# Subtracting the low parts of the later projection weights on GpSimd instead of VectorE

## The chip, the cores and the metric

One core of one Trainium2 chip. The metric is the device time of one execution of the whole program in microseconds; the kernel before took 951.87 us, the median of three runs from 950.09 to 952.92 us.

## The reference

One layer of a bidirectional hybrid trunk over 640 tokens of width 1024: 128 context tokens and 512 latent tokens. Each token is modulated by adaLN and goes through one combined input projection, whose columns feed three groups: A, differential attention with four heads; B, an HGRN2 gated linear recurrence with four heads and chunks of 64 tokens in both directions; C, grouped-query attention. The results pass one output projection, a LayerNorm, a squared-ReLU MLP and a second LayerNorm.

```
z = (x * (1 + sc1) + sh1) @ w_in            # 640 x 1024 times 1024 x 3328
qa, ka, va, qb, fb_f, fb_b, ib, gb, qc, kc, vc = split(z)
mixed = concat(diff_attention(qa, ka, va), hgrn2(qb, fb_f, fb_b, ib) * silu(gb), gqa(qc, kc, vc))
x = LN(ALPHA * x + g1 * (mixed @ w_out))
x = LN(ALPHA * x + g2 * (relu((x * (1 + sc2) + sh2) @ w_ff1) ** 2 @ w_ff2))
```

The change touches only how the weights `w_in` are prepared for the projections.

## The kernel before

All projections are done in split precision. A float32 operand `src` is split into a high part, a copy rounded to float32r, and a low part, `src - high` (`split`, lines 89 to 91): ScalarE makes the high part, VectorE subtracts. A product is then three matmuls (`mm3`, lines 126 to 130): high times high, high times low, low times high. The activations lie split in `xh` and `xl`.

`wslots` (lines 93 to 124) brings weights in. For each slot it takes a raw buffer `wr`, of which there are two (`NWR`), and a low and a high buffer `wl`, `wh`, of which there are five each (`NWS`); it issues the loads on SP's queue (line 108), and calls `split` on the whole slot, or with `swap=True` on pieces of 256 columns that are rearranged on the way. A raw buffer is free for the next load when both the copy and the subtraction have read it; a high and a low buffer when the matmuls have. A slot holds 768 or 1024 columns per partition.

The callers in the order of the work. In the start stage `first_load` brings `wfq` (gates of the recurrence and first queries), while the adaLN vectors are made. Then `tok_gemm` (line 418) makes the token-major `ib` and `gb`, two slots of 1024 each; `load("fb2")` brings `wfb`, two slots with four pieces of 256 each; `load("q1")` brings `wq`, one slot of 1024. `a_gemm` (line 735) makes queries, keys and values of one head of group A from `wa`, four slots of 768 per head, 16 in all; `c_gemm` (line 845) those of group C from `wc`, four slots of 1024. Later stages load `wo`, `wf` and `wg` by the same function.

Beside the projections runs the recurrence: `gates` and `b_scores` are long sequences of VectorE and ScalarE work over `b_b`, `b_k`, `b_d` and `b_lqk` with small matmuls (`pslv`, `psl`, `pskht`) between, `b_state` a chain of small VectorE steps (line 560). The `ada` calls load further pieces of the adaLN weight and need a ScalarE copy between two matmuls (line 145). The attention follows as a pipeline of units.

The calls from line 1038 on are in an order written out by hand, with projection tiles between the stages of the recurrence. But that order is a priority: a planner lays out the instructions of each engine from these priorities, from the waits for data and free buffers, and from its own estimate of each instruction's cost. Only inside `manual_schedule` blocks is TensorE's order as written. Each engine then takes its instructions strictly in the order laid out. SP's queue holds the loads. GpSimd has little to do: fills of constants and of query tiles, and transfers (small inputs, caches, states in and out, bias rows, context outputs), which it issues itself; such an instruction waits in the queue for what it needs, and what is behind it waits too.

Of the kernel before, what the change touches and what calls it, by code (L numbers as in the profile page):

```python
# [15 lines left out]
ALU = mybir.AluOpType  # L16
# [3 lines left out]
P = 128  # L20
# [33 lines left out]
COL_QA, COL_KA, COL_VA = 0, 512, 1024  # L54
COL_QB, COL_FF, COL_FB, COL_IB = 1536, 1792, 2048, 2304
COL_C = 2816


def f32(ap):
    return ap.bitcast(F32)  # L60
# [3 lines left out]
def hybrid_layer_kernel(ctx: ExitStack, tc: tile.TileContext, T):  # L64
    nc = tc.nc
    V, A, G, PE = nc.vector, nc.scalar, nc.gpsimd, nc.tensor
# [19 lines left out]
    xl = ctile("xl", [P, NK, NTOK], F32R)  # L86


    def split(hi, lo, src):
        A.copy(hi, src)  # L90
        V.tensor_tensor(lo, src, f32(hi), op=ALU.subtract)  # L91

    def wslots(name, src, cols, kper, row0=0, nslot=None, swap=False):


        n = sum(w for _, w in cols)
        nslot = nslot or NK // kper
        out = []
        for s in range(nslot):
            raw = wp.tile([P, kper * n], F32, tag="wr", name=f"{name}_r{s}", bufs=NWR)  # L100
            lo = wp.tile([P, kper * n], F32R, tag="wl", name=f"{name}_l{s}", bufs=NWS)
            hi = wp.tile([P, kper * n], F32R, tag="wh", name=f"{name}_h{s}", bufs=NWS)
            lv = lo.rearrange("p (k n) -> p k n", n=n)
            rv = raw.rearrange("p (k n) -> p k n", n=n)
            off = 0
            r0 = row0 + s * kper * P
            for c0, w in cols:
                nc.sync.dma_start(
                    rv[:, :, off : off + w],
                    src[r0 : r0 + kper * P, c0 : c0 + w].rearrange("(k p) n -> p k n", p=P),  # L110
                )
                off += w
            hv = hi.rearrange("p (k n) -> p k n", n=n)
            if swap:
                for k in range(kper):
                    h_, l_ = (v[:, k, 0:256].rearrange("p (h d c) -> p d h c", d=2, h=2) for v in (hv, lv))
                    split(h_, l_, rv[:, k, 0:256].rearrange("p (d h c) -> p d h c", d=2, h=2))
                if n > 256:
                    split(hv[:, :, 256:n], lv[:, :, 256:n], rv[:, :, 256:n])
            else:  # L120
                split(hi, lo, raw)
            for k in range(kper):
                out.append((hv[:, k, :], lv[:, k, :]))
        return out

    def mm3(ps, s, m, start, stop):

        PE.matmul(ps, s[0], m[0], start=start, stop=False)  # L128
        PE.matmul(ps, s[0], m[1], start=False, stop=False)  # L129
        PE.matmul(ps, s[1], m[0], start=False, stop=stop)  # L130

    def xcols(k, c0, n):
        return (xh[:, k, c0 : c0 + n], xl[:, k, c0 : c0 + n])
# [150 lines left out]
    def ps_mm(name):  # L284
        return pps.tile([P, 512], F32, tag="mm", name=name, bufs=2)
# [7 lines left out]
    def p1t(tag, shape, dtype=F32, bufs=1, name=None):  # L293
        return p1.tile(shape, dtype, tag=tag, name=name or tag, bufs=bufs)
# [121 lines left out]
        V.tensor_tensor(q, q, t, op=ALU.mult)  # L416

    def tok_gemm(name, c0, dst, eng):
        wk = wslots(f"w{name}", T["w_in"], ((c0, 256),), 4)

        def tile_(t):
            ps = ps_mm(f"ps{name}{t}")
            for k in range(NK):
                mm3(ps[:, 0:256], xcols(k, t * P, P), wk[k], k == 0, k == NK - 1)
            eng(dst[:, t, :], ps[:, 0:256])

        return tile_
# [200 lines left out]
    def new_grp(name, par, ck, cv):  # L628
        g = Grp()
        g.name = name  # L630
        g.par = par
        g.qtags = ("a_q0", "a_q1", "b_b1", "b_k1") if name == "C" else ("a_q0", "a_q1", "b_k0", "b_k1")
        g.ltags = ("a_kl", "u6", "u3", "b_b0")
        g.src = (ck, cv)
        g.z = []
        return g
# [7 lines left out]
    def z_tile(g, t):  # L644
        if t == 0:
            return p1t("a_zc", [P, 512], bufs=1, name=f"z{g.name}0")
        if g.par:
            return p1t(f"u{6 + t}", [P, 512], name=f"z{g.name}{t}")
        return p1t("a_z", [P, 512], bufs=4, name=f"z{g.name}{t}")
# [85 lines left out]
    def a_gemm(h):  # L735
        g = new_grp(f"A{h}", h % 2, T["cache_a_k"][:, h * P : (h + 1) * P], T["cache_a_v"][:, h * P : (h + 1) * P])
        g.kcol = P
        g.vcol = 256
        wk = wslots(f"wa{h}", T["w_in"], [(c + h * P, P) for c in (COL_QA, COL_KA, COL_VA)], 2)

        def tile_(t):
            ps = ps_mm(f"psA{h}{t}")
            for k in range(NK):
                mm3(ps[:, 0:384], xcols(k, t * P, P), wk[k], k == 0, k == NK - 1)
            if t == 0:
                z = z_tile(g, t)
                A.copy(z[:, 0:384], ps[:, 0:384])
                nc.gpsimd.dma_start(T["new_a_k"][:, h * P : (h + 1) * P], z[:, P : 2 * P])
                nc.gpsimd.dma_start(T["new_a_v"][:, h * P : (h + 1) * P], z[:, 2 * P : 3 * P])
            else:  # L750
                z = z_tile(g, t)
                rope(z[:, 0:256], ps[:, 0:256], z[:, 256:512], t - 1, 4)
                A.copy(z[:, 256:384], ps[:, 256:384])
            g.z.append(z)

        g.tiles = [lambda t=t: tile_(t) for t in range(NT)]
        return g
# [87 lines left out]
    def c_gemm():  # L845
        g = new_grp("C", 0, T["cache_c_k"], T["cache_c_v"])
        g.kcol = 256
        g.vcol = 384
        wk = wslots("wc", T["w_in"], ((COL_C, 512),), 2)

        def tile_(t):
            ps = ps_mm(f"psC{t}")
            for k in range(NK):
                mm3(ps, xcols(k, t * P, P), wk[k], k == 0, k == NK - 1)
            sq = p1t("tmp", [P, GMAX], bufs=3, name=f"csq{t}")
            ss = p1t("c_ss", [P, 6], bufs=2, name=f"css{t}")
            A.activation(sq, ps[:, 0:384], AF.Square)
            V.tensor_reduce(ss, sq.rearrange("p (g v) -> p g v", v=HD), axis=AX.X, op=ALU.add)
            A.activation(ss, ss, AF.Ln, scale=1.0 / HD, bias=eps)
            A.activation(ss, ss, AF.Exp, scale=-0.5)  # L860
            if t == 0:
                z = z_tile(g, t)
                zn = z[:, 0:384]
            else:
                z = z_tile(g, t)
                zt = p1t("tmp", [P, GMAX], bufs=3, name=f"zn{t}")
                zn = zt[:, 0:384]
            V.tensor_tensor(zn.rearrange("p (g v) -> p g v", v=HD), ps[:, 0:384].rearrange("p (g v) -> p g v", v=HD),
                            ss.rearrange("p (g o) -> p g o", o=1).to_broadcast([P, 6, HD]), op=ALU.mult)
            for lo, n, gg in ((0, 4, qng), (256, 2, kng)):  # L870
                zz = zn[:, lo : lo + n * HD].rearrange("p (g v) -> p g v", v=HD)
                V.tensor_tensor(zz, zz, gg.rearrange("p (o v) -> p o v", o=1).to_broadcast([P, n, HD]), op=ALU.mult)
            if t == 0:
                A.copy(z[:, 384:512], ps[:, 384:512])
                nc.gpsimd.dma_start(T["new_c_k"], z[:, 256:384])
                nc.gpsimd.dma_start(T["new_c_v"], z[:, 384:512])
            else:
                rt = p1t("tmp", [P, GMAX], bufs=3, name=f"rt{t}")
                rope(z[:, 0:384], zn, rt, t - 1, 6)
                A.copy(z[:, 384:512], ps[:, 384:512])  # L880
            g.z.append(z)

        g.tiles = [lambda t=t: tile_(t) for t in range(NT)]
        return g
# [105 lines left out]
    gr, parts, tok, wks = {}, {}, {}, {}  # L990
# [3 lines left out]

    def load(name):
        if name == "q1":
            wks[name] = wslots("wq1", T["w_in"], ((COL_QB + P, P),), 8)
        elif name == "fb2":
            wks[name] = wslots("wfb2", T["w_in"], ((COL_FF + P, P), (COL_FB + P, P)), 4, swap=True)
        elif name == "ib":  # L1000
            tok[name] = tok_gemm("ib", COL_IB, ib, A.copy)
        elif name == "gb":
            tok[name] = tok_gemm("gb", COL_IB + 256, gb, A.copy)
        else:
            gr[0] = a_gemm(0)
# [87 lines left out]
    for h in range(NHA):  # L1093
        for t in range(1, NT):
            n = h * nu + t - 1
# [42 lines left out]
    for t in range(1, NT):  # L1138
        for j in range(4):
            n = NHA * nu + (t - 1) * 4 + j  # L1140
# [96 lines left out]
    for n in range(2):  # L1237
        g1r = gate_rows("g1", n)
        wk = wslots(f"wo{n}", T["w_out"], ((n * 512, 512),), 2)
# [64 lines left out]
    for n in range(2):  # L1304
# [3 lines left out]
        for s in range(NF // 2):  # L1308
            wk = wslots(f"wg{n}_{s}", T["w_ff2"], ((n * 512, 512),), 2, row0=s * 256, nslot=1)
# [99 lines left out]
```

## Time and profile before

| | us |
|---|---|
| median of three runs | 951.87 |
| the profiled execution | 952.96 |
| its span in the trace | 951.2 |
| TensorE (PE) busy, share of the span | 96% |
| VectorE (DVE) busy | 60% |
| ScalarE (ACT) busy | 45% |
| GpSimd (POOL) busy | 6% |

The profiled execution took 1.76 us more than its span, work that lies before the first and behind the last instruction of the trace, and 1.09 us more than the median. A busy share is an average over stages with different limits; the MLP, which takes the second half of the span, is nearly all matmuls. Times of single rows are counted from the start of the span.

### The profile page before, as it was taken

The numbers are of one execution on the slowest core, as the hardware profiler recorded it, in microseconds if no ns is written. First come the engines' busy times: TensorE is split into PE (matmuls) and PEld (weight loads), VectorE is DVE, ScalarE is ACT, GpSimd is POOL, SyncE is SP. The second block draws the span as 40 slices with busy tenths as digits, with TensorE's granted clock in tenths as the row PEclk, the third lists the DMA queues.
The fourth block names the chain that finished last, engine by engine and source line by source line (L and its number), as shares of the span: only waits on it lengthen the run. The fifth ranks groups of instructions, "written<-read, shape, count | busy, mean of one in ns | idle before, by whom it ended". The sixth has DMA issues, their size and how long they took to land.

```text
span 951.2 us, 15540 instructions
## 1 busy us (share of the span) xinstructions
PE 912.9 (96%) x6133; PEld 792.2 (83%) x6133; DVE 573.6 (60%) x1123; ACT 432.7 (45%) x916; POOL 53.5 (6%) x108
## 2 busy tenths in 40 slices
PE   6989898999999998999999999999999999999996
PEld 4778886889889786678899999999998888888884
DVE  2378998988876888873794313243236343563448
ACT  3566675466664657651583212222225333243320
POOL 2200010210100000001000000000000000000000
PEclk9998999999999998999999999999999999999998
DMA  9951525433021320113223234342122222142102
GB/s 260 290 157 54 157 86 162 108 92 94 19 78 39 117 65 13 68 45 133 89 68 111 61 95 133 121 125 73 61 90 84 72 68 88 34 152 80 67 23 88
DMA packets 95752, 90.82 MB, mean 95 GB/s; under 512 B 5792, under 2 KB 81280, under 8 KB 95680
## 3 DMA queue, kind: packets, MB, share of 16 engines
q1 hardware_dynamic: 91936, 82.50, 28.9%
q0 software_dynamic: 3552, 7.27, 2.5%
q8 instruction: 48, 0.79, 0.3%
q14 instruction: 24, 0.20, 0.1%
q10 hardware_dynamic: 192, 0.08, 0.0%
HBM read 86.41 MB, written 3.41 MB: 94 GB/s over the span
## 4 chain that ended last, share of the span: by engine, by line
PE 80%; DVE 11%; ACT 3%; DMA 3%; issue 1%; SPq 1%; DVEq 0%; ACTq 0%
PE psf L1271 8%; PE psy L130 8%; PE psf L1272 8%; PE psf L1273 8%; PE psy L129 8%; PE psy L128 8%; PE psA L129 2%; PE psA L130 2%; PE psavA L730 2%; PE psA L128 2%; PE pswo L130 2%; PE pswo L129 2%; PE pswo L128 2%; DVE b_st L560 2%; PE psavC L952 2%
## 5 line engine op out<-in xcount | busy, mean ns | idle before, releaser
L1271 PE MATMUL psf<-xh,wf_h 128*128 128x320 f32 x512 | 158.7, 310 | 0.0
L1272 PE MATMUL psf<-xl,wf_h 128*128 128x320 f32 x512 | 158.1, 309 | 0.0
L1273 PE MATMUL psf<-xh,wf_l 128*128 128x320 f32 x512 | 158.1, 309 | 0.0
L130 PE MATMUL psy<-wg_h,xl 128*128 128x512 f32 x320 | 127.7, 399 | 0.0
L129 PE MATMUL psy<-wg_l,xh 128*128 128x512 f32 x320 | 126.1, 394 | 0.0
L128 PE MATMUL psy<-wg_h,xh 128*128 128x512 f32 x320 | 125.5, 392 | 0.0
L91 DVE TENSOR_TENSOR xl<-hid,xh 128x640 fp32r<-128x640 f32 x64 | 52.1, 824 | 86.5 <-ACT xh L90 86.5
L90 ACT CAST xh<-hid 128x640 fp32r<-128x640 f32 x64 | 45.6, 727 | 121.7 <-PE psy L129 116.2
L1271 PEld LDWEIGHTS psf<-xh,wf_h 128*128 128x128 f32 x512 | 96.3, 188 | 1.7 <-issue 1.2
L1272 PEld LDWEIGHTS psf<-xl,wf_h 128*128 128x128 f32 x512 | 96.3, 188 | 0.0
L1273 PEld LDWEIGHTS psf<-xh,wf_l 128*128 128x128 f32 x512 | 96.3, 188 | 0.0
L1276 DVE TENSOR_TENSOR hid<-hid,psf 128x320 f32<-128x320 f32 x64 | 31.1, 486 | 106.5 <-ACT hid L1275 106.4
L1275 ACT ACTIVATE hid<-psf 128x320 f32<-128x320 f32 x64 | 28.0, 438 | 119.9 <-PE psf L1273 119.9
L129 PEld LDWEIGHTS psy<-wg_l,xh 128*128 128x128 f32 x320 | 60.1, 188 | 15.6
L128 PEld LDWEIGHTS psy<-wg_h,xh 128*128 128x128 f32 x320 | 60.1, 188 | 14.3
L130 PEld LDWEIGHTS psy<-wg_h,xl 128*128 128x128 f32 x320 | 60.1, 188 | 13.7
L91 DVE TENSOR_TENSOR wf_l<-wf_r,wf_h 128x1024 fp32r<-128x1024 f32 x32 | 39.2, 1224 | 37.5 <-ACT wf_h L90 37.5
L128 PE MATMUL psA<-wa_h,xh 128*128 128x384 f32 x160 | 55.2, 346 | 0.0
L130 PE MATMUL psA<-wa_h,xl 128*128 128x384 f32 x160 | 54.9, 344 | 0.0
L129 PE MATMUL psA<-wa_l,xh 128*128 128x384 f32 x160 | 54.7, 343 | 0.0
L90 ACT CAST wf_h<-wf_r 128x1024 fp32r<-128x1024 f32 x32 | 33.7, 1054 | 32.8 <-PE psf L1272 28.4
L91 DVE TENSOR_TENSOR wg_l<-wg_r,wg_h 128x1024 fp32r<-128x1024 f32 x32 | 39.2, 1224 | 7.1 <-ACT wg_h L90 4.5
(475 smaller groups left out, 1897.2 us busy)
## 6 DMA issues: line engine op xcount, KB each, us to landing
wad<-in_w_ada SPq DMA_DIRECT2D x32, 512.0 KB, 4.8
wf_r<-in_w_ff SPq DMA_DIRECT2D x32, 512.0 KB, 3.9
wg_r<-in_w_ff SPq DMA_DIRECT2D x32, 512.0 KB, 3.6
adaw<-in_w_ada SPq DMA_DIRECT2D x32, 256.0 KB, 5.4
wa_r<-in_w_in SPq DMA_DIRECT2D x48, 128.0 KB, 2.9
wo_r<-in_w_out SPq DMA_DIRECT2D x8, 512.0 KB, 3.7
x<-in_x_sample SPq DMA_DIRECT2D x8, 256.0 KB, 4.9
wc_r<-in_w_in SPq DMA_DIRECT2D x4, 512.0 KB, 3.7
```

Of the source, the lines that this page charges most:

```text
L90: A.copy(hi, src)
L91: V.tensor_tensor(lo, src, f32(hi), op=ALU.subtract)
L128: PE.matmul(ps, s[0], m[0], start=start, stop=False)
L129: PE.matmul(ps, s[0], m[1], start=False, stop=False)
L130: PE.matmul(ps, s[1], m[0], start=False, stop=stop)
L560: V.scalar_tensor_tensor(dst, st[r, c, :], dec[r, c : c + 1], u(r, c), op0=ALU.mult, op1=ALU.add)
L730: PE.matmul(po, pT[:, c, :], vals(g, c, c0, n), start=(c == 0), stop=(c == NKC - 1))
L1271: PE.matmul(ps[:, 0:HALF], h, xh[:, k, sl], start=(k == 0), stop=False)
L1272: PE.matmul(ps[:, 0:HALF], h, xl[:, k, sl], start=False, stop=False)
L1273: PE.matmul(ps[:, 0:HALF], l, xh[:, k, sl], start=False, stop=(k == NK - 1))
L1275: A.activation(hs, ps[:, 0:HALF], AF.Relu)
L1276: V.tensor_tensor(hs, hs, ps[:, 0:HALF], op=ALU.mult)
```

## The change

`split` and `wslots` get a parameter `eng`, the engine of the subtraction; without it VectorE is used as before. The five calls, for `ib` and `gb` together, `wa`, `wc`, `wq` and `wfb`, pass GpSimd. The high part is made on ScalarE as before, and `wfq`, `wo`, `wf`, `wg` and the activations are split as before.

```diff
-    def split(hi, lo, src):
+    def split(hi, lo, src, eng=None):
         A.copy(hi, src)
-        V.tensor_tensor(lo, src, f32(hi), op=ALU.subtract)
+        (eng or V).tensor_tensor(lo, src, f32(hi), op=ALU.subtract)
...
-    def wslots(name, src, cols, kper, row0=0, nslot=None, swap=False):
+    def wslots(name, src, cols, kper, row0=0, nslot=None, swap=False, eng=None):
...
-                    split(h_, l_, rv[:, k, 0:256].rearrange("p (d h c) -> p d h c", d=2, h=2))
+                    split(h_, l_, rv[:, k, 0:256].rearrange("p (d h c) -> p d h c", d=2, h=2), eng)
                 if n > 256:
-                    split(hv[:, :, 256:n], lv[:, :, 256:n], rv[:, :, 256:n])
+                    split(hv[:, :, 256:n], lv[:, :, 256:n], rv[:, :, 256:n], eng)
             else:
-                split(hi, lo, raw)
+                split(hi, lo, raw, eng)
...
-        wk = wslots(f"w{name}", T["w_in"], ((c0, 256),), 4)
+        wk = wslots(f"w{name}", T["w_in"], ((c0, 256),), 4, eng=G)
...
-        wk = wslots(f"wa{h}", T["w_in"], [(c + h * P, P) for c in (COL_QA, COL_KA, COL_VA)], 2)
+        wk = wslots(f"wa{h}", T["w_in"], [(c + h * P, P) for c in (COL_QA, COL_KA, COL_VA)], 2, eng=G)
...
-        wk = wslots("wc", T["w_in"], ((COL_C, 512),), 2)
+        wk = wslots("wc", T["w_in"], ((COL_C, 512),), 2, eng=G)
...
-            wks[name] = wslots("wq1", T["w_in"], ((COL_QB + P, P),), 8)
+            wks[name] = wslots("wq1", T["w_in"], ((COL_QB + P, P),), 8, eng=G)
         elif name == "fb2":
-            wks[name] = wslots("wfb2", T["w_in"], ((COL_FF + P, P), (COL_FB + P, P)), 4, swap=True)
+            wks[name] = wslots("wfb2", T["w_in"], ((COL_FF + P, P), (COL_FB + P, P)), 4, swap=True, eng=G)
```

## Rows read from the trace of the kernel before

**Rows 1.** The page's engine totals: busy us, share of the span, instructions.

```profile
PE 912.9 (96%) x6133; PEld 792.2 (83%) x6133; DVE 573.6 (60%) x1123; ACT 432.7 (45%) x916; POOL 53.5 (6%) x108
```

**Rows 2.** Busy time by stretch: length, each engine's busy us, granted clock, DMA share, GB/s.

```profile
95.00:120.00 25.00, 22.57 (x217) 20.66 (x216) 24.17 (x64) 16.65 (x44) 1.51 (x2) 0.93 0.54 167
...
245.00:270.00 25.00, 24.56 (x163) 22.64 (x161) 19.75 (x43) 12.17 (x36) 1.43 (x2) 1.00 0.10 28
```

**Rows 3.** What TensorE waited for: us in total, times, longest us.

```profile
PE pskht L488 <- DVE b_kq L485: 3.1, 1, 3.1
PE psl L499 <- DVE b_k L528: 2.4, 1, 2.4
PE psada L976 <- ACT ada L145: 2.2, 1, 2.2
```

**Rows 4.** Subtractions of line 91 that move: duration ns min/median/max, first and last start.

```profile
L91 DVE TENSOR_TENSOR wa_l<-wa_r,wa_h x16: 936/951/960, 143.2 to 279.7; 128x768 fp32r<-128x768 f32 x16
...
L91 DVE TENSOR_TENSOR wfb_l<-wfb_r,wfb_h x8: 415/418/425, 63.4 to 85.9; 128x256 fp32r<-128x256 f32 x8
...
L91 DVE TENSOR_TENSOR wc_l<-wc_r,wc_h x4: 1218/1221/1227, 284.6 to 318.4; 128x1024 fp32r<-128x1024 f32 x4
L91 DVE TENSOR_TENSOR wib_l<-wib_r,wib_h x2: 1224/1224/1225, 52.3 to 54.8; 128x1024 fp32r<-128x1024 f32 x2
L91 DVE TENSOR_TENSOR wgb_l<-wgb_r,wgb_h x2: 1209/1213/1217, 95.8 to 103.5; 128x1024 fp32r<-128x1024 f32 x2
L91 DVE TENSOR_TENSOR wq_l<-wq_r,wq_h x1: 1215/1215/1215, 91.6 to 91.6; 128x1024 fp32r<-128x1024 f32 x1
```

**Rows 5.** Groups of GpSimd's instructions by form: busy us, mean ns, idle before.

```profile
L432 POOL MEMSET b_lqk<- 128x768 f32 x3 | 2.2, 739 | 22.2 <-PE psada_s L143 22.2
...
L254 POOL CAST masks<-mf 128x256 uint8<-128x256 f32 x1 | 0.4, 396 | 1.8 <-DMA mf<-in_k_masks 1.8
...
L960 POOL MEMSET brow<- 128x256 f32 x1 | 0.3, 330 | 0.0
```

**Rows 6.** Timelines of GpSimd, and of VectorE at 110 us: start, us, instruction.

```profile
110.29 0.77 POOL L569 DMA_DIRECT2D out_new_state_fwd<-b_stn  x1 [24.24 <-DVE b_stn L560]
111.05 0.75 POOL L570 DMA_DIRECT2D out_new_state_bwd<-b_stn  x1
...
136.88 0.55 POOL L569 DMA_DIRECT2D out_new_state_fwd<-b_stn  x1 [4.51 <-DVE b_stn L560]
...
110.34 0.61 DVE L388 TENSOR_SCALAR mixed<-mixed,lbt 128x640 f32<-128x640 f32 x1
```

**Rows 7.** The chain that ended last, 52 to 71 us: start, us, what.

```profile
52.29 1.24 DVE wib_l L91
53.54 0.37 SPq L108
...
57.23 5.68 DMA wfb_r<-in_w_in
...
65.03 0.42 DVE wfb_l L91
...
70.62 0.33 DVE wfb_l L91
```

**Rows 8.** What VectorE waited for, 75 to 95 us, then 145 to 175 us.

```profile
DVE b_att L538 <- ACT b_att L537: 1.5, 1, 1.5
DVE b_att L539 <- PE psl L499: 1.0, 1, 1.0
...
DVE sc L978 <- ACT wa_h L90: 1.4, 1, 1.4
DVE ada L147 <- PE psadag L143: 1.3, 1, 1.3
DVE sc L978 <- PE psada L976: 0.8, 2, 0.6
```

**Rows 9.** A weight load of TensorE's that waited for a low part.

```profile
PEld psC L129 <- DVE wc_l L91: 0.2, 1, 0.2
```

**Rows 10.** Busy time by stretch, 112.5 to 115 us; columns as in rows 2.

```profile
112.50:115.00 2.50, 2.50 (x11) 2.50 (x11) 2.47 (x5) 2.35 (x8) 0.00 (x0) 0.50 0.03 7
```

## The prediction

> **What bounds the kernel now.** The page's engine totals come first [rows 1]: TensorE is busy 912.9 of 951.2 us, VectorE 60%, GpSimd 6%. So all that a change off TensorE can win is in the 38 us in which TensorE has nothing to do, and in stretches in which its clock is lowered. The average hides that the work has stages, so the second view is the busy time by stretch [rows 2]. From 95 to 120 us, in the HGRN2 part, VectorE is busy 24.17 of 25 us while TensorE has 2.4 us of gaps: there VectorE sets the pace. From 245 to 270 us, in the attention part, TensorE is busy 24.56 of 25 and VectorE 19.75: there TensorE sets it, and a lighter VectorE buys next to nothing. The third view is what TensorE waits for [rows 3]: 3.1 us for `b_kq` at 71 us, 2.4 us for `b_k` at 111 us, both from VectorE, and 2.2 us for ScalarE's `ada` copy, which stands behind a ScalarE instruction that VectorE feeds. These three are what the change can shorten or lengthen.
>
> **What moves.** The subtractions of line 91 for six weight names go from VectorE to GpSimd [rows 4]: 2 of `wib` and 2 of `wgb` and 1 of `wq` and 4 of `wc` at 1.21 to 1.22 us each, 8 of `wfb` at 0.42, 16 of `wa` at 0.95. That is 9 x 1.22 + 8 x 0.42 + 16 x 0.95 = 29.5 us off VectorE. The cast to the high part stays on ScalarE, the loads stay on SP's queue, no instruction is added. The subtractions of `wfq`, `wo`, `wf`, `wg` and of the activations stay on VectorE.
>
> **What one costs on GpSimd.** No subtraction ran there before, so I bound it. Two fills give the cost of one pass [rows 5]: (739 - 330) / 512 = 0.80 ns an element, 0.125 us fixed. One pass over 1024 elements is 0.94 us, the lower bound. Two reads and a write done as three passes are 2.58 us for 1024, 1.97 for 768, 0.74 for 256, the upper bound. The cast of 256 elements at 396 ns shows that a read beside a write is cheaper than a pass of its own, but it writes single bytes; I take the upper bound. So each result comes about twice as late after its cast as on VectorE, if nothing stands before it. [...]
>
> **What it costs VectorE while it runs.** This decides the sign, and no row shows it, since GpSimd never read two tiles before. The lower bound is nothing. The upper bound is that VectorE stands still for the whole subtraction, as nearly all that it runs in these stretches reads two SBUF tiles or streams one at speed. The nearest row is a small one [rows 6]: GpSimd's two output transfers of a state take 0.77 and 0.75 us beside VectorE's `TENSOR_SCALAR` at 110.34 us, but 0.55 us at 136.88. The two engines do get in each other's way; I take the upper bound, in which a subtraction of 1.22 us on VectorE turns into a stop of 2.58. [...]
>
> **The sum, in three places.**
>
> *A, 52 to 71 us.* The chain of waits [rows 7] runs through this change: `wib_l` ends at 53.54, frees a raw buffer (there are two, `NWR`), and at that moment SP issues the `wfb` load; SP's constants follow in order, the other `wfb` loads go at 57.23 and land 5.68 us later, and everything to the 3.1 us wait hangs on that. The subtraction takes 2.58 instead of 1.22, so this starts 1.36 us later. Two `wfb_l` subtractions, 0.42 and 0.33 us, leave the chain. Net +0.6 us. Behind the waiting SP instruction stand the constants and the `ada` weight loads, which are needed later.
>
> *C, 72 to 112 us.* Off VectorE: 5 x 0.42 of `wfb`, 1.22 of `wq`, 2 x 1.21 of `wgb`, together 5.7 us. Added as stops: 5 x 0.74 + 3 x 2.58 = 11.4 us. VectorE's own idle time there can swallow 1.5 + 1.0 us [rows 8]. Net 11.4 - 2.5 - 5.7 = +3.2 us, and all of it lengthens TensorE's 2.4 us wait, since TensorE has run out of filler matmuls by then.
>
> *D, 141 to 157 us.* Four `wa` subtractions: off 4 x 0.95 = 3.8, added 4 x 1.97 = 7.9, idle to swallow it 1.4 + 1.3 + 0.8 = 3.5 [rows 8]. Net +0.6 us on the chain that feeds the `ada` copy.
>
> Elsewhere I cost the change at nothing: the other twelve `wa` and the four `wc` run beside an attention stage whose matmuls cover both VectorE's relief and its stops. If that cover fails, the price is a low part that reaches TensorE late: 1.36 us for a `wc`, 1.02 for a `wa`. One row shows that this is near, a weight load that already waits 0.2 us for `wc_l` [rows 9].
>
> GpSimd's own queue is nearly empty (53.5 us in all [rows 1]). What now stands behind a subtraction are fills for the query tiles and transfers of caches, states and bias rows, each up to 2.6 us later, which has slack. The reverse, a subtraction behind a GpSimd instruction that itself waits, can cost far more (one waited 24.24 us [rows 6]); the planner orders queues by its own estimate of when things are ready, so I leave it to the range. So do I with the changed order of all engines: the planner sees other costs and will place matmuls differently after 52 us.
>
> Sum: 0.6 + 3.2 + 0.6 = +4.4 us on the profiled execution's 952.96 us, 957.4. The median of the runs is 1.09 us below that execution, so **956.3 us**.
>
> **Rivals.**
> *VectorE is not held at all (faster).* [...] With A's +0.6: -5.1 us, 946.7. For it: VectorE is the pacing engine there and GpSimd idle. Against: the lengthened transfers. It begins to decide where the stops of C fall under what is removed and swallowed, 5.7 + 2.5 = 8.2 us of the 11.4. Chance 0.34.
>
> *VectorE is held only while GpSimd reads.* Two passes of three: C's stops are 7.6 us, 0.6 less than what is removed and swallowed; D comes out covered; A's +0.6 stays. Sum 0.0, 951.9. Chance 0.24. What would be late next is the same `b_k`, hardly moved.
>
> *The held case with late low parts.* The forecast plus one `wc` and one `wa` late, 1.36 + 1.02: 958.7. Chance 0.10; the forecast by itself 0.32.
>
> **How the numbers follow.** About 0.3%, 2.9 us, can be told from no change. Slower by more: 0.32 + 0.10 = 0.42. Within it: 0.24. Faster: 0.34. Low end: the first rival, with a GpSimd subtraction at its one-pass bound so that A turns from +0.6 to -1.0, 945.1; I say 945. High end: 958.7 and the 1.25 us of lowered clock twice more, after the two waits that grow, 961.2; I say 961. Both signs hold most of the chance; the forecast's own range is 954 to 961.
>
> **What would show it.** Right: VectorE's two-input instructions between 85 and 105 us (scans, `b_lqk`) grow by up to 2.6 us wherever a GpSimd subtraction runs beside them; the wait of TensorE for `b_k` near 111 us grows from 2.4 to over 5; the `wfb` loads leave SP some 1.4 us later; a GpSimd subtraction of 1024 takes 2 us or more. Wrong: VectorE's instructions keep their lengths beside GpSimd's subtractions, its busy total falls by the full 29.5 us, and the `b_k` wait is gone; or the planner's order changes so much that TensorE's gaps lie in other places.

## The result, and the profile after

The changed kernel takes **978.1 us** (median of four runs, 976.9 to 980.3) against 952.4 before in the same job: ratio 1.0274, 95% interval 1.0249 to 1.0299. It is slower, as forecast, but by 25.7 us where the sum had 4.4, and outside the range of 945 to 961.

The page's totals of the changed kernel answer to [rows 1].

```profile
PE 920.8 (94%) x6133; PEld 798.3 (82%) x6133; DVE 571.1 (58%) x1090; ACT 435.0 (45%) x916; POOL 114.5 (12%) x141
```

33 instructions and 29.5 us of subtractions have left VectorE, and its busy time fell by 2.5 us: 573.6 - 29.5 = 544.1, so 27.0 us came back. Summed one by one, the VectorE instructions that stayed are 23.6 us longer; the rest is that instructions in a row overlap a little, which the busy time counts once: 47.3 us of VectorE's instructions overlap before, 43.9 after. The span grew by 25.1 us, of which TensorE has 7.9 more busy and 17.2 more idle.

Next, the moved subtractions but for `wq_l`, by source line and operation (duration min/median/max in ns, first and last start), against [rows 4].

```profile
L91 POOL TENSOR_TENSOR wa_l<-wa_r,wa_h x16: 1804/1824/2407, 150.4 to 298.7; 128x768 fp32r<-128x768 f32 x16
L91 POOL TENSOR_TENSOR wfb_l<-wfb_r,wfb_h x8: 719/862/1916, 65.6 to 77.7; 128x256 fp32r<-128x256 f32 x8
L91 POOL TENSOR_TENSOR wc_l<-wc_r,wc_h x4: 2334/2384/2432, 300.5 to 338.4; 128x1024 fp32r<-128x1024 f32 x4
L91 POOL TENSOR_TENSOR wib_l<-wib_r,wib_h x2: 2382/2386/2389, 52.7 to 58.4; 128x1024 fp32r<-128x1024 f32 x2
L91 POOL TENSOR_TENSOR wgb_l<-wgb_r,wgb_h x2: 2687/2698/2708, 94.5 to 99.3; 128x1024 fp32r<-128x1024 f32 x2
```

The timelines of GpSimd and of VectorE from 90 to 104 us show where that comes from (start, us, instruction).

```profile
90.73 2.39 POOL L91 TENSOR_TENSOR wq_l<-wq_r,wq_h 128x1024 fp32r<-128x1024 f32 x1
94.48 2.71 POOL L91 TENSOR_TENSOR wgb_l<-wgb_r,wgb_h 128x1024 fp32r<-128x1024 f32 x1 [1.35 <-ACT wgb_h L90]
99.33 2.69 POOL L91 TENSOR_TENSOR wgb_l<-wgb_r,wgb_h 128x1024 fp32r<-128x1024 f32 x1 [2.14 <-ACT wgb_h L90]
...
90.76 2.72 DVE L388 TENSOR_SCALAR b_b<-b_b,lbt 128x640 f32<-128x640 f32 x1
95.12 2.42 DVE L390 TENSOR_SCALAR b_k<-b_b 128x640 f32<-128x640 f32 x1
98.34 1.48 DVE L392 TENSOR_TENSOR_SCAN b_b<-scanm,b_b 64x640 f32<-64x640 f32 x1
100.50 2.87 DVE L393 TENSOR_TENSOR_SCAN b_b<-scanm,b_b 64x640 f32<-64x640 f32 x1
```

Read them in pairs. Line 388 takes 0.61 us in [rows 6]; here it starts 0.03 us after `wq_l` and ends 0.36 us behind it. Line 390, 0.49 us in the kernel before, ends 0.35 us behind the first `wgb_l`. The scan of line 392 is under way when the second `wgb_l` starts and keeps its 1.48 us; the same scan at line 393, which starts during that subtraction, takes 2.87 and ends 1.35 us behind it.

What TensorE waits for has changed places too (columns as in [rows 3]).

```profile
PE psl L499 <- DVE b_stn L560: 4.9, 2, 4.1
PE pskht L488 <- DVE b_kq L485: 4.7, 2, 4.0
PE psqA L678 <- DVE zA L623: 3.5, 3, 2.2
PE psqA L678 <- DVE lam L355: 3.0, 1, 3.0
...
PE psada L976 <- ACT ada L145: 1.4, 1, 1.4
```

The `psl` products near 120 us no longer wait for `b_k` but for the state steps of line 560; two waits of the first attention head are new. VectorE's queue isn't the old one less 33 instructions: the planner gave every engine another order. First products by stage, before and after: `pskht` 71.3 and 75.6 us, `psq` 104.3 and 112.5, `psA` 152.7 and 165.5, `psC` 313.0 and 337.5, `pswo` 426.1 and 451.3. So 12.8 us are lost before the first attention product, 11.7 between it and `psC`, 0.7 up to `pswo`, nothing behind it.

The first stretch of [rows 2] and the one behind the 4.1 us wait for `b_stn` (columns as there):

```profile
95.00:120.00 25.00, 19.85 (x192) 18.56 (x192) 23.75 (x54) 13.88 (x33) 4.87 (x2) 0.99 0.43 136
...
120.00:125.00 5.00, 4.26 (x29) 4.17 (x30) 4.86 (x12) 2.17 (x7) 1.50 (x2) 0.50 0.04 10
```

From 95 to 120 us TensorE lacks 5.2 us of 25 where it lacked 2.4, and VectorE is as full as before. Behind the long wait the granted clock is 0.50, as it was in [rows 10] behind a shorter one; some of TensorE's extra busy time comes from there: a `psq` product of the changed kernel takes 0.47 us at 123 us and 0.31 at 115 us, where the clock is 1.00.

### The profile page after: what moved, and what is told of

Same layout as the page of the kernel before. It is cut to its first block, busy times and chain, and to the rows that moved or that the text cites. A ratio compares the mean times of both kernels' runs of the same rounds, so it can differ in the third digit from the quotient of the medians.

```text
span 976.3 us, 15559 instructions
## 1 busy us (share of the span) xinstructions
PE 920.8 (94%) x6133; PEld 798.3 (82%) x6133; DVE 571.1 (58%) x1090; ACT 435.0 (45%) x916; POOL 114.5 (12%) x141
## 4 chain that ended last, share of the span: by engine, by line
PE 74%; DVE 11%; issue 6%; ACT 3%; DMA 3%; SPq 1%; POOL 1%; DVEq 0%; ACTq 0%; POOLq 0%
PE psf L1271 8%; PE psy L130 8%; PE psf L1272 8%; PE psf L1273 8%; PE psy L129 8%; PE psy L128 8%; PE psavA L730 2%; PE pswo L130 2%; PE pswo L129 2%; PE pswo L128 2%; PE psavC L952 2%; PE psA L128 2%; PE psA L130 1%; PE psA L129 1%; DVE b_st L560 1%
## 5 line engine op out<-in xcount | busy, mean ns | idle before, releaser
L91 DVE TENSOR_TENSOR wg_l<-wg_r,wg_h 128x1024 fp32r<-128x1024 f32 x32 | 39.2, 1224 | 7.3 <-ACT wg_h L90 4.5
```

The source lines that it names most:

```text
L91: (eng or V).tensor_tensor(lo, src, f32(hi), op=ALU.subtract)
```

## The experiments

Two things changed at once: the engine of 33 instructions, and everybody's order. Both kernels consist of the same instructions, so either can be held to the other's order: each instruction of an engine gets a plain order edge to its predecessor in the wanted list (shortened).

```
+    for i in ORDER:                        # the other kernel's order
+        ins = trace[i]
+        if ins.engine in last:
+            tc.add_manual_dep(ins, last[ins.engine].name, no_sync)
+        last[ins.engine] = ins
```

"Old order" is that of the kernel before, "new order" that of the changed kernel. Losses are differences of medians within one job (the kernel before had 952.3 to 953.5 there).

| run | order | low parts on | median us | ratio, 95% interval | loss us | VectorE busy |
|---|---|---|---|---|---|---|
| before | old | VectorE | 952.4 | | | 573.6 |
| r1 | old | GpSimd | 966.8 | 1.0150 (1.0129-1.0171) | 13.6 | 572.2 |
| r2 | new | VectorE | 971.7 | 1.0203 (1.0181-1.0225) | 18.5 | 575.0 |
| r4 | old | GpSimd, hardly reading | 956.0 | 1.0027 (1.0011-1.0043) | 3.0 | 551.2 |
| r5 | new | GpSimd, hardly reading | 961.1 | 1.0087 (1.0064-1.0109) | 8.0 | 550.3 |
| changed | new | GpSimd | 978.1 | 1.0274 (1.0249-1.0299) | 25.7 | 571.1 |

**r1 and r2: engine or order.**

> The changed kernel (all 33 subtractions on GpSimd), but with every engine's instructions held in the order that the planner had given the kernel before. The changed kernel lost 25.7 us (952.4 to 978.1). Theory 1, the engine alone costs it (VectorE's instructions stretch beside GpSimd's subtractions, low parts and raw buffers come later): the loss stays, 972 to 982 us. Theory 2, the planner's new order of the other instructions costs most: 953 to 962 us, with VectorE's busy time still near 571 us, since the stretch would stay and only stop mattering. If both matter, between 962 and 972.

> The kernel before (all subtractions on VectorE, none on GpSimd), but with every engine's instructions held in the order that the planner gave the changed kernel. Theory 1, engine alone: 950 to 955 us, as the kernel before. Theory 2, order: 968 to 980 us, with TensorE waiting at the same places as in the changed kernel (the subtraction's own state chain b_stn, psqA, pskht) although no VectorE instruction is stretched.

r1 comes out between its two theories, r2 within that of the order. Each alone costs, and together less than their sum, 25.7 against 32.1. Measured from the old order, the engine is 13.6 us and the order another 12.1. r2 has the changed kernel's waits with no subtraction on GpSimd.

```profile
PE psl L499 <- DVE b_stn L560: 4.9, 2, 4.1
PE psqA L678 <- DVE lam L355: 4.5, 1, 4.5
```

These two are the order's. r1 has neither; there `ada` and `b_lqk` lead.

```profile
PE psada L976 <- ACT ada L145: 6.2, 1, 6.2
...
PE pslv L499 <- DVE b_lqk L515: 2.8, 2, 2.2
```

**r3: the pairs by themselves.**

```
+    def y_sub(o): G.tensor_tensor(o, ga, gb, op=ALU.subtract)   # also memset, copy
+    def x_sub(o): V.tensor_tensor(o, va, vb, op=ALU.subtract)   # and six other forms
```

> None of the layer is computed: this kernel only runs six VectorE instructions of each of seven forms, first alone, then beside a stream of GpSimd subtractions (128x1024, both inputs and the output in SBUF), beside GpSimd memsets and beside GpSimd copies; the outputs are filled with zeros. Theory 'held for the whole subtraction' (the upper bound of the prediction): a VectorE instruction with two SBUF inputs takes up to its own time plus about 2.4 us beside the subtractions, and a form with one input or with its input in PSUM keeps its length. Theory 'not held': every form keeps its length within 0.05 us. Theory 'held while reading only': the added time is near 1.6 us of each 2.4. [...]

VectorE's groups by tile (ns min/median/max, first and last start), then the timelines of both engines.

```profile
L82 DVE TENSOR_TENSOR vo_x_sub_alone<-va,vb x6: 1159/1224/1224, 6.8 to 13.9; 128x1024 f32<-128x1024 f32 x6
L82 DVE TENSOR_TENSOR vo_x_sub_y_set<-va,vb x6: 1224/1224/1224, 54.9 to 61.1; 128x1024 f32<-128x1024 f32 x6
L82 DVE TENSOR_TENSOR vo_x_sub_y_sub<-va,vb x6: 1224/3245/3245, 15.7 to 28.1; 128x1024 f32<-128x1024 f32 x6
L94 DVE TENSOR_TENSOR_SCAN vo_x_scan_y_sub<-va,vb x6: 1492/3446/3448, 312.7 to 328.1; 128x640 f32<-128x640 f32 x6
L91 DVE TENSOR_SCALAR vo_x_imm_alone<-va x6: 493/1200/1202, 229.5 to 235.0; 128x640 f32<-128x640 f32 x6
L91 DVE TENSOR_SCALAR vo_x_imm_y_sub<-va x6: 494/2951/3393, 236.1 to 247.2; 128x640 f32<-128x640 f32 x6
```

```profile
3.28 12.04 POOL L106 MEMSET go_x_sub_y_set<- 128x1024 f32 x12
8.93 6.19 DVE L82 TENSOR_TENSOR vo_x_sub_alone<-va,vb 128x1024 f32<-128x1024 f32 x5
...
21.24 2.42 POOL L103 TENSOR_TENSOR go_x_sub_y_sub<-ga,gb 128x1024 f32<-128x1024 f32 x1
23.61 0.95 POOL L106 MEMSET go_x_sub_y_set<- 128x1024 f32 x1
24.52 2.42 POOL L103 TENSOR_TENSOR go_x_sub_y_sub<-ga,gb 128x1024 f32<-128x1024 f32 x1
...
229.94 4.65 POOL L106 MEMSET go_x_imm_y_set<- 128x1024 f32 x4 [1.02 <-ACT t L125]
...
390.50 2.35 POOL L103 TENSOR_TENSOR go_x_psum_y_sub<-ga,gb 128x1024 f32<-128x1024 f32 x1
390.51 4.30 DVE L97 TENSOR_TENSOR vo_x_psum_y_copy<-pt,vb 128x512 f32<-128x512 f32 x6
```

The planner mixed the streams, so the labels don't say what ran beside what; the starts do. The subtractions called "alone" from 8.93 us run beside GpSimd's memsets, those called "y_set" from 54.9 us beside an idle GpSimd: 1224 ns both. Beside GpSimd's subtractions VectorE gets one instruction through for each of GpSimd's: it lasts 3245 ns, 2.02 us more, from 0.26 us behind the subtraction's start, and GpSimd's period (21.24 to 24.52, with a memset in it) is 3.28 us. The scan (1491 ns undisturbed) grows by 1.95 us. The form that reads PSUM keeps its length beside the same subtractions (4.30 us for six from 390.51, under 0.7 each at any time). So "held for the whole subtraction" stands, 2.02 of the 2.33 us that a subtraction takes beside an idle VectorE; "held while reading", with 1.6, falls.

The one-input `TENSOR_SCALAR`, which the prediction's list of signs didn't name and which r3's own theory took to keep its length, is held too: 0.49 us beside an idle GpSimd, up to 3.39 beside its subtractions. It is held by memsets as well: of the six called "alone", the four that run beside GpSimd's memsets from 229.94 us take 1.20 us, and the memsets that meet them 1.18 instead of 0.95. So memsets on GpSimd, which only write, leave VectorE's two-input forms as they are (subtraction 1224 ns, product 824, scan 1491 beside them) and hold this one-input form.

**r4 and r5: GpSimd as long busy, but hardly reading.** Here the low parts are mostly zeros.

```
-        eng.tensor_tensor(lo, src, f32(hi), op=ALU.subtract)
+        eng.tensor_tensor(lo[..., 0:2], src[..., 0:2], f32(hi)[..., 0:2], op=ALU.subtract)
+        eng.memset(f32(lo), 0.0)            # twice
+        eng.tensor_tensor(lo[..., 0:2], src[..., 0:2], f32(hi)[..., 0:2], op=ALU.subtract)
```

> The old order, as in r1, but each GpSimd subtraction is replaced by a tiny one (2 columns of each row), two memsets of the low part and a tiny one again: GpSimd is busy for about as long (2.1 us where the subtraction takes 2.4), low parts and raw buffers are released about as late, but GpSimd hardly reads SBUF; r3 showed VectorE unchanged beside memsets. The low parts are then mostly zeros. Theory 'VectorE held': the 13.6 us of r1 vanish, 948 to 955 us, and VectorE's busy time falls to about 545 us. Theory 'low parts and raw buffers late, GpSimd's queue': 963 to 967 us, as r1.

> The same replacement in the order that the planner gave the changed kernel (978.1 us with the real subtractions; 971.7 with the subtractions on VectorE). Theory 'VectorE held, and the order costs by itself': 964 to 971 us: the holding is gone, the order's loss stays. Theory 'the order costs only because the subtractions sit badly in it': 950 to 957 us. Theory 'late low parts': about 977 us.

```profile
PE 909.2 (95%) x6133; PEld 788.2 (83%) x6133; DVE 551.2 (58%) x1090; ACT 432.7 (45%) x916; POOL 117.5 (12%) x240
...
57.65 2.33 DVE L332 TENSOR_SCALAR sel<-ident,selw 128x128 fp32r<-128x128 f32 x2
...
57.65 2.10 POOL L432 MEMSET b_lqk<- 128x768 f32 x3
```

GpSimd is busy for 117.5 us against 113.4 in r1, VectorE 21.0 us less, and 10.6 of r1's 13.6 us are gone. r4 is 1.0 us above the range of its first theory, and r5, at 961.1, lies between its first two. "VectorE unchanged beside memsets" holds for two-input forms only, so r4 isn't free of holding: VectorE's total is 7.1 us above the 544.1 that the subtractions leave, where the text expected about 545, and 4.9 of that are longer instructions. Most of these are early, two one-input `sel` instructions that take 2.33 us beside the kernel's own `b_lqk` fills where they took 0.48 before. So the holding by subtractions is at least 10.6 us in the old order and 17.7 in the new one, and the new order by itself is 5. The 3.0 us left in r4 are what late low parts and buffers cost, with the holding left, less what VectorE's relief gives; the three weren't measured apart. r4 does say that with low parts as late as that, 22.4 us less of VectorE's time don't make the kernel faster.

**r6, r7, r9: which stage.** r6 moves `wa` and `wc` only, r7 the other three call sites only, r9 is r6 with r4's replacement, all in the old order. The counts in two texts below are off: it is 20 subtractions (16 of `wa`) and 13.

> The old order; of the 33 subtractions only those of the attention stage (12 of wa, 4 of wc) are on GpSimd, the 17 of wib, wfb, wq and wgb stay on VectorE. The prediction counted 0.6 us for these 16 (953.7 us here). Rival: the stage doesn't cover the holding; r1's milestones lose 5 to 7 us between the first wa product and the last wc product, so 958 to 960 us.

> The old order; only the 17 subtractions of wib, wfb, wq and wgb are on GpSimd, those of wa and wc stay on VectorE. The prediction counted 3.8 us (957 us here). Rival, by r1's milestones: 7 to 8 us are lost before the first wa product, so 960 to 962 us. If r6 and r7 add up to r1's 13.6 us, the two stages cost independently.

> As r6 (old order; only the 20 subtractions of wa and wc on GpSimd, 961.1 us), with each of them replaced as in r4 by two tiny subtractions and two memsets, so that GpSimd is as long busy and hardly reads. The low parts of wa and wc are then mostly zeros. Theory 'VectorE held': most of r6's 8.0 us vanish, 952 to 956 us. Theory 'low parts and raw buffers late' in this stage: 959 to 961 us.

r7: 957.0 us, +4.0 (ratio 1.0044, 1.0028 to 1.0059), as the prediction counted. r6: 961.1, +8.0 (1.0088, 1.0065 to 1.0110), 1.1 above its rival's range. r9: 956.4, +2.9 by the medians (1.0045, 1.0027 to 1.0062), 0.4 above its first theory's range. The attention stage is the dearer one, and some 5 of its 8 us are the holding (4 by the ratios). The sum of r6 and r7, 12.0, is within the noise of r1's 13.6. One place shows how it gets to TensorE: first the kernel before, then r6, timelines of three engines near 143 us.

```profile
142.22 1.02 DVE L511 TENSOR_TENSOR b_d<-mixed 128x384 f32<-128x384 f32 x2
...
144.55 0.37 ACT L145 COPY ada<-psada 128x256 f32<-128x256 f32 x1
```

```profile
142.79 4.50 DVE L511 TENSOR_TENSOR b_d<-mixed 128x384 f32<-128x384 f32 x2
...
142.49 2.05 POOL L91 TENSOR_TENSOR wa_l<-wa_r,wa_h 128x768 fp32r<-128x768 f32 x1 [0.97 <-ACT wa_h L90]
...
145.05 1.82 POOL L91 TENSOR_TENSOR wa_l<-wa_r,wa_h 128x768 fp32r<-128x768 f32 x1
...
145.04 0.45 ACT L512 ACTIVATE b_d<-b_d,sgn 128x192 f32<-128x192 f32 x1 [1.69 <-DVE b_d L511]
...
146.73 0.37 ACT L145 COPY ada<-psada 128x256 f32<-128x256 f32 x1
```

Two subtractions `b_d` stand one behind the other on VectorE, and each meets one `wa_l`: 1.02 us become 4.50. ScalarE's next instruction waits 1.69 us for the first, the `ada` copy stands behind it in ScalarE's queue and comes 2.18 us later, and TensorE's wait for `ada` goes from 2.2 to 4.1 us. The first `psA` product starts 3.0 us later than before.

Further on the loss grows where one head of attention follows another. What TensorE waits for (columns as in [rows 3]), in the kernel before, in r6 (with two rows of its timelines) and in r9:

```profile
PE psqA L678 <- DVE zA L623: 0.4, 1, 0.4
```

```profile
PE psqA L678 <- DVE zA L623: 2.1, 2, 1.2
...
PE pssA L705 <- DVE k0A L669: 1.2, 1, 1.2
...
317.05 2.19 DVE L623 TENSOR_TENSOR zA<-zA 128x256 f32<-128x256 f32 x1
...
314.27 4.69 POOL L91 TENSOR_TENSOR wc_l<-wc_r,wc_h 128x1024 fp32r<-128x1024 f32 x2 [12.16 <-ACT wc_h L90]
```

```profile
PE psC L129 <- POOL wc_l L1397: 1.1, 1, 1.1
...
PE psA L129 <- POOL wa_l L1397: 1.0, 1, 1.0
```

The step `zA` takes 0.43 us at this place in the kernel before, 2.19 beside `wc_l`, and the first products of the head wait for it. In r9 the wait for `zA` is 0.4 us again, and TensorE waits 1.1 and 1.0 us for a low part: most of r9's 2.9.

**r11 and r12: the size of a hold, and VectorE's time without one.**

```
+    for c in range(0, m, m // 4):           # r11: four quarters on GpSimd (shortened)
+        eng.tensor_tensor(lo[..., c : c + w], src[..., c : c + w], f32(hi)[..., c : c + w], op=ALU.subtract)
```

```
     V.tensor_tensor(lo, src, f32(hi), op=ALU.subtract)
+    V.tensor_tensor(lo, src, f32(hi), op=ALU.subtract)   # r12: twice on VectorE
```

> As r1 (all 33 subtractions on GpSimd, the old order, 966.8 us), but each subtraction of 1024 or 768 columns is four of 256 or 192, one behind the other; those of 256 stay. Theory 'a VectorE instruction waits for one whole GpSimd instruction': it now waits for about 0.7 us in place of up to 2.4 and slips in between two quarters, so VectorE's added time falls and the kernel takes 956 to 962 us. Rival 'the two share a path and the sum of their reading counts': 966 to 970 us, since GpSimd is as long busy or longer.

> The kernel before (subtractions on VectorE, the old order), with each of the 33 subtractions done twice in a row on VectorE: 29.5 us more of VectorE's time in the places where the subtractions stand, about as much as GpSimd's holding adds in r1 (28 us). Theory 'VectorE is late wherever it is held, and its time in these stages is the bound': 962 to 970 us. Rival 'VectorE has room there, and what costs in r1 is that the holding falls on instructions that others wait for': 953 to 957 us.

r11: 961.2 us (ratio 1.0090, 1.0064 to 1.0116), 5.6 us better than r1, though GpSimd is busy 130.9 us instead of 113.4; VectorE's total falls to 565.2. A hold that is over sooner costs less, and the rival of a shared sum falls. r12: 972.5 us (1.0214, 1.0179 to 1.0250), above both its ranges, VectorE 602.4 us. There 28.8 more us of VectorE's time cost 20.0, 0.7 us for each. So more time on VectorE in these places does go to the end; but r12's low parts also come one subtraction later (TensorE waits 1.7 us for `wa_l`), and that part wasn't taken apart. r1 adds nearly as much by holding (25.2, summed one by one) and takes the 29.5 us of subtractions away, and still loses 13.6: what it takes away pays little of it back.

**r8 and r10: filling single waits.** r8 mends the two waits of the changed kernel that are the order's; r10 does one such edit in the kernel before.

```
 PE (r10):  - psl x16, psq x16     + psq x16, psl x16
 PE (r8):   - psl x16, psq x22     + psq x22, psl x16
 DVE (r8):  - b_st x7, zA/lam x9   + zA/lam x9, b_st x7
```

> The changed kernel with its real subtractions on GpSimd and in its own order, but for two places. The 16 products psl, before which TensorE waits 4.1 us for the state steps b_stn, come 22 psq products later on TensorE; and nine instructions that the first attention queries need (zA and lam) come ahead of the last 7 of the 16 state steps on VectorE, where TensorE waited 3.0 us. Theory 'what the new order costs over the old one (11.3 us with the subtractions on GpSimd) lies in such places': 978.1 minus 4 to 8, so 970 to 974 us. Rival 'the waits only move, since VectorE is behind by as much': 976 to 979 us, with a new wait just behind each place.

> The kernel before (subtractions on VectorE), in its own order but for one place: the 16 products psl, before which TensorE waits 2.4 us for b_k near 111 us and after which its granted clock falls to 0.50, come 16 psq products later. If the wait is filled and the clock doesn't fall there: 948.5 to 951 us. If the time only moves to the wait behind it: 952 to 954 us, as before.

r8 takes 979.2 us (1.0273, 1.0259 to 1.0287), the same as the changed kernel; my theory fell. r10 takes 953.7 (0.9999, 0.9985 to 1.0013). r8's list of TensorE's waits says why: the time has gone next door.

```profile
PE pskht L488 <- DVE b_kq L485: 6.4, 4, 4.0
...
PE psl L499 <- DVE b_k L528: 3.6, 1, 3.6
PE psgb L128 <- ACT b_q L409: 3.2, 1, 3.2
```

In r10 the 2.4 us for `b_k` are gone and the waits for `b_kq` are 6.8 us in place of 3.1; the granted clock is at 0.50 again, from 118 to 121 us. A wait of TensorE's names who came last, not what the time hangs on.

**r13 and r14: whose order.** Both with all low parts on GpSimd; r13 is r1 with the queues of GpSimd and SP in the new order, r14 the changed kernel with these two in the old.

> As r1 (all 33 subtractions on GpSimd; VectorE, ScalarE and TensorE in the old order, 966.8 us), but the queues of GpSimd and of SP run in the order that the planner gave the changed kernel: the first low part stands ahead of the fills of b_lqk and of the state loads, the query fills and output transfers stand between other subtractions. Theory 'the new order costs through the queues': 974 to 978 us, as the changed kernel. Rival 'through the compute engines': 965 to 969 us.

> The counterpart: the changed kernel (978.1 us) with the queues of GpSimd and SP in the old order, VectorE, ScalarE and TensorE in the new one. Theory 'queues': 966 to 970 us. Rival 'compute engines': 976 to 980 us. If neither of r13 and r14 moves by 3 us or more, the cost lies in how the orders of the engines fit each other.

r13: 968.4 us (1.0159, 1.0136 to 1.0181), r14: 985.5 (1.0356, 1.0334 to 1.0379). Losses are 16.0 and 33.1 us: the two queues in the new order cost 2.4 us beside the old order of the rest, which the noise can hide, and save 7.4 beside the new; r14 is above both its ranges. So the order's loss sits with VectorE, ScalarE and TensorE. Their orders were not exchanged one at a time; which of their placements costs the 5 to 12 us stays open.

## Why the prediction was right and wrong

**Right: what a subtraction costs on GpSimd.** Taken 2.58, 1.97 and 0.74 us, measured 2.33, 1.80 and 0.72 at best. Where nothing held it r3 shows 2.33 for 1024. VectorE holds GpSimd as well: 2.69 for `wgb_l`, 1.92 for one `wfb_l`.

**Right: VectorE is held for the whole of it.** r3 (1224 ns become 3245), r4 (10.6 of r1's 13.6 us gone) and r11 (5.6 us less with quarters) show it, against the two rivals that had 0.58 of the chance.

**Right in size, C by luck: A and C.** The other `wfb` loads left SP at 58.72 us in the changed kernel, 1.49 later than in [rows 7] (taken: 1.36), and at 58.12 in r7, 0.89 later. r7 measures A and C together, 4.0 us where the steps had 0.6 + 3.2 = 3.8. The sign by which the loss was to show was wrong: the `b_k` wait did not grow to 5 us; in r7 `b_lqk` (2.2 us) and `b_kq` (4.4 in all) took it, and in the changed kernel `b_k` stands at 1.1. Nor does C's sum hold with what was measured: the VectorE instructions that stand between 72 and 112 us in the kernel before grew by 7.9 us in r7, where the prediction took a stop for each subtraction, 11.4. Its own terms then give 7.9 - 2.5 - 5.7 = -0.3. What cost was where a stop fell: a pair of `b_lqk` steps beside the second `wgb_l` took 2.65 us in place of 0.58, and TensorE waited for that (r7's timeline and waits):

```profile
103.76 2.65 DVE L515 TENSOR_TENSOR b_lqk<-b_k,b_d 64x128 f32<-64x128 f32 x2
...
PE pslv L499 <- DVE b_lqk L515: 2.2, 1, 2.2
```

**Wrong: D and "elsewhere".** "The other twelve `wa` and the four `wc` run beside an attention stage whose matmuls cover both VectorE's relief and its stops", with 0.6 us for the first four. r6 measured 8.0 us for these 20. The idle time that was to swallow the stops in D, 3.5 us in [rows 8], lay mostly at 151 to 162 us, and the first stops fell on `b_d` at 142, ahead of it: +3.0 us instead of +0.6 at the first `psA`. Part of it is won back, since TensorE waits 1.4 us for a weight at 161 us in the kernel before: the first `psqA` starts at 193.8 us before and at 196.0 in r6. The other 6 us come where the prediction had nothing. A stage in which TensorE is 24.56 of 25 us busy [rows 2] is not covered at the changes of head; at those TensorE waits for a short chain on VectorE and ScalarE, and a stop on that chain counts, as `zA` shows. The price put on a failed cover, late low parts for 1.36 + 1.02 us, is near the 2.1 us of such waits in r9; it left out the holding, some 5 us here. This mis-sized term is 7.4 us of the missing 21.3.

**Wrong: the order left to the range.** "So do I with the changed order of all engines", and then the high end had two lowered clocks in it and no order. No run shows the 1.25 us counted for each of the two, an estimate from the 2.5 us at half the clock in [rows 10]; in stretches of 2.5 us the granted clock is at 0.50 for 41.0 us in the changed kernel and for 20.5 before, the end of the span behind the matmuls left out. The order cost 12.1 us on top of r1. With the 1.6 us by which r1 exceeds r6 and r7 together (12.0 against 13.6; r1's interval alone is 2.0 us to each side), the two steps make up the miss: 7.4 + 12.1 + 1.6 = 21.1 of 21.3, and r7's 0.2 is the rest. Which placements in the new order cost this stays open; r13 and r14 leave those of VectorE, ScalarE and TensorE.

**The first rival would have been wrong too.** It gave 946.7 if VectorE were not held. No run shows its -5.1 us: r10, without the `b_k` wait, takes as long as before (953.7), and r4, which is close to the rival's case, takes 956.0: the waits for `b_k` (2.0 us) and `b_kq` (3.7 in two) are still there with 22.4 us less on VectorE. Whether relief pays where low parts come no later wasn't tried.

## What to carry to other kernels

Before moving an elementwise subtraction to an idle GpSimd, ask what VectorE runs beside it: in r3, beside GpSimd subtractions with two SBUF inputs, each VectorE form tried whose inputs all lie in SBUF was held (subtraction 1224 ns to 3245, product 824 to 2849, scan 1491 to 3446, `TENSOR_SCALAR` 0.49 us to 3.39), while the PSUM reader kept its 0.69 us, and short GpSimd pieces cost less than long ones (13.6 us down to 8.7, r11). Replacing GpSimd's reading by fills didn't free all of VectorE: the one-input form was held by fills too (0.49 us to 1.20). A stage in which TensorE is 98% busy wasn't covered where its chain changes hands (8.0 us in r6). And where a planner orders the engines, a changed engine is a new program: hold the order fixed in one experiment and the engines in another before reading any wait as a cause.

## What the runs showed that was not expected

VectorE's time paid in one direction only as far as it was tried: 28.8 us more cost 20.0 (r12), 22.4 us less with low parts about as late as in the change gained nothing (r4, +3.0). The order that the planner chose for the changed engines is worse by 5 us even where VectorE is hardly held (r5 against r4), and by 18.5 with the subtractions back on VectorE (r2). And a 0.95 us memset on GpSimd leaves VectorE's two-input subtraction at 1224 ns, where a subtraction on GpSimd makes it 3245; but it holds VectorE's one-input `TENSOR_SCALAR` (0.49 us to 1.20), and is itself lengthened by it (0.95 to 1.18).
